# A fourth group in the second Q/K unit, a fifth in w_out's first and a seventh in w_down's last, with four more raw places and a later return of h

## The chip, the cores and the metric

The kernel runs on one core of one Trainium2 chip. The metric is the device time of one execution in microseconds (us), as the median of several runs; lower is better. PE is the matrix engine (PEld its weight loads), DVE the vector engine, ACT the scalar engine, POOL GpSimd and SP the sync engine, which here only issues transfers.

## The reference, cut to what matters

One layer of a hybrid decoder, on 256 tokens of width 2048, in float32:

```python
def hybrid_mixer(u, w_in, ..., w_out):
    proj = jnp.einsum('bsd,de->bse', u, w_in)
    z, xbc, dt_raw, q, k, v = jnp.split(proj, IN_SPLITS, axis=-1)
    ...
    y_mix = jnp.concatenate([y_ssm, y_att], axis=-1)
    return jnp.einsum('bse,ed->bsd', y_mix, w_out)

def squared_relu_mlp(u, w_up, w_down):
    hdn = jax.nn.relu(jnp.einsum('bsd,df->bsf', u, w_up))
    return jnp.einsum('bsf,fd->bsd', hdn * hdn, w_down)

h = h + rmsnorm(hybrid_mixer(rmsnorm(h, ...), ...), norm_mix_post[i])
h = h + rmsnorm(squared_relu_mlp(rmsnorm(h, ...), ...), norm_mlp_post[i])
```

y_ssm comes from a state-space scan (SSD, 32 heads), y_att from an attention of 16 heads. w_in is 2048 x 12320, w_out 4096 x 2048, w_up 2048 x 8192, w_down 8192 x 2048. The work around the change is in the products with w_in (the columns of q, k and v), w_out and w_down.

## The kernel before, in words

**Products in three parts.** PE multiplies in fp32r, which is less exact than float32. So each operand is split into a high part and a rest, x = hi + lo, and a product of float32 becomes three matmuls: hi by hi, hi by lo, lo by hi. The activations stay in SBUF, split, with the features on the partitions (`u` for the layer's input, called ua, ub and uc in a profile; `sh`, `sl` for y_ssm; `ah`, `al` for y_att, and later sh and ah hold the MLP's inner activations). The weights come from DRAM in raw tiles of 256 rows x 512 columns (512 KB), a "block" of k each: `fetch` and `fetch_next` (L149, L201) issue the load on SP's queue, `split` (L140) has ACT write hi (L144) and DVE write lo = raw - hi (L145). There are five pairs of hi and lo (BUFS). Raw tiles lie in a ring of four buffers (RAWS), to which `room["raw"]` adds places that other data do not need at that time; `room["turn"]` counts through the ring.

**Units and groups.** `unit` (L436) computes 256 tokens x two column blocks of 512, over a list of k blocks, in an order that is written out by hand. A *plain* block takes, for each column block, one raw tile and 2 token tiles x 2 k x 3 = 12 matmuls of 512 columns (`row_tile`, L325 to L327), 24 in all. A block *by seven* (a "group": `seven`, L372) uses Strassen's way of multiplying 2 x 2 blocks with seven products in place of eight: 7 x 3 = 21 matmuls (L408 to L410) into four more accumulators (`more`). It needs sums of weight tiles, which DVE adds (L249: e, of two tiles' size, and t4, of half), each split like a raw tile, so that four tiles are split (a, e, b and t, the last of half size); and sums of activations, which `sums_of_acts` (L354) makes once for each block of k and keeps in `room["sums"]`: four DVE additions (L365 to L368) and a split into hi and lo. In the tables of blocks this sum stands ahead of the block before the group. Of the second column block a group needs the sum of its two rows too: for w_out, w_up and w_down a pair of transfers on POOL's queue adds them up in DRAM ahead of time (`next_pair`, L264; the second transfer accumulates; five places, four ahead), and SP loads the sum; for w_in DVE adds them in place (raw<-raw). Behind a unit's last group a `combine` adds the four extra accumulators to the results, and a few plain blocks (`last`) close the unit, one column block after the other.

**Order.** The engines' queues are in program order. The loads and splits of weights have a high priority, so that they are placed as early as their buffers allow; `split_in_line` and `add_in_line` keep ACT's and DVE's part of them in the order of the blocks. `waiting` holds generators (attention, sums, copies), of which `pump` takes a step behind each block's column block.

**The three stages.** (1) The second Q/K unit, `keys_by_tokens(1, ...)`, takes heads 4 to 7 of q and k as its two column blocks. It starts when the SSD is done, whose memory becomes `ah` and `al` (16 feature blocks each). Their second halves hold the sums of activations at first; the first halves are empty until attention writes y_att there, behind the first V unit (`heads`). That V unit, `two_values(0, ...)`, comes next, with groups 1, 3, 5 and 6. (2) w_out's first unit takes columns 0 to 1023, blocks 5 to 15 (the first five are done before); its sums of activations are kept for the second unit, which uses block 9 too. (3) w_down's last unit, the second half of the inner features by columns 1024 to 2047, ends the kernel. In both of w_down's last units the layer's h lies in DRAM (`h_d`), so that its places (`ha`, `hb`) can hold raw tiles: the ring is 4 + 2 (uc) + 3 (ha) + 1 (hb) = 10 places in the unit before and 4 + 2 in the last. At the last unit's start `copies` brings h back on ACT's queue (8 transfers of 128 x 512, one a step), and `load_wpost` loads two of the norm's weights. Behind the last unit (`complete`, `finish`) h gets the MLP's normed output added and is stored.

Of the kernel before, what the change touches and what calls it, by code (L numbers as in the profile page):

```python
# [16 lines left out]
P = 128  # L17
S = 256
# [36 lines left out]
QK_SEVENS = (1, 3, 5)  # L55
# [22 lines left out]
def hymba_layer(ctx: ExitStack, tc: tile.TileContext, x, norm_mix_pre, w_in, conv_w, conv_b, dt_bias, a_log,  # L78
# [34 lines left out]
    def part(k):  # L113
        return (sh, sl, k) if k < NK else (att["h"], att["l"], k - NK)
# [74 lines left out]
    def beside_up(raws, turn):  # L189

        room["sums"] = [v[:, k:k + KB] for k in range(NK // 2, NK, KB) for v in (ah, al)]
# [67 lines left out]
    def plan(name, src, n, order, by_seven):  # L259

        orders[name, n] = order_of(order, by_seven)
        pairs.extend((src, n * NB, k) for k in order if k in by_seven)
# [162 lines left out]
    plan("out", w_out, 0, range(EARLY, 14), (6, 8, 10, 12))  # L425
# [8 lines left out]
    plan(("down", 1), w_downs[1], 2, (0, 1, 3, 2, 6, 4, 8, 5, 11, 7, 13, 9), (3, 6, 8, 11, 13, 9))  # L434
# [409 lines left out]
    def attention(ap, h, qT, kT, v):  # L844
# [39 lines left out]
        split(ah[:, h:h + 2], al[:, h:h + 2], o)  # L884
# [94 lines left out]
    ah = att["h"] = bigr.tile([P, NK, S], F32R, name="ah")  # L979
    al = att["l"] = bigr.tile([P, NK, S], F32R, name="al")  # L980
    ap_ = ExitStack()
    ap = ap_.enter_context(tc.tile_pool(name="ap", bufs=2, side="right", reuse_waits="tile"))
    room["sums"] = [v[:, k:k + KB] for k in range(NK // 2, NK, KB) for v in (ah, al)]
    room["raw"], room["turn"], room["acts"] = [], 0, act_u
# [5 lines left out]
    qk.append(keys_by_tokens(1, (0, 2, 1, 4, 3, 7, 5), (6,), *eight))  # L990
    vs = two_values(0, *eight[::-1])
    heads(0, *qk[0], vs[0])
# [233 lines left out]
    nc.scalar.activation(cp.tile([P, 1], F32, name="mean", bufs=2), al[:, NK - 1, 0:1].bitcast(F32), AF.Sqrt, scale=0.0, bias=ones[:, 0:1])  # L1226
# [4 lines left out]
    def new_h():  # L1231
        hs[:] = [hp.tile([P, NT, n * NB], F32, name=name) for n, name in ((3, "ha"), (1, "hb"))]
# [108 lines left out]
    def copies(dst, src, step):  # L1341

        for n in range(4):
# [82 lines left out]
    a, b = hp.tile([P, 3 * KB, NB], F32, name="ha"), hp.tile([P, KB, NB], F32, name="hb")  # L1426
    in_u = room["raw"]
    room["raw"] = [*in_u, *(a[:, k:k + KB] for k in range(0, 3 * KB, KB)), b]
# [5 lines left out]
    for n in (2, 3):  # L1434
        load_wpost(norm_mlp_post, n)
    new_h()
    room["raw"], room["turn"], room["chain"] = in_u, 0, False
    waiting.append(copies(of_h, in_dram, 1))
    unit(w_downs[1], 2, orders[("down", 1), 2], (10, 12, 14, 15), more, acc,
         lambda x: combine_onto(2, x), LAG_DOWN, (complete(2), finish))  # L1440
# [23 lines left out]
```

## Time and profile before

| what | us |
|---|---|
| median of 3 runs | 1460.41 (1460.25 to 1460.97) |
| the profiled execution | 1460.92 |
| its span, first to last instruction | 1459.0 |
| splits of raw tiles on ACT (L144, hi<-raw), 412, busy | 431.1 |
| the same on DVE (L145, lo<-raw,hi), 412, busy | 501.7 |
| raw tiles of w_in by SP, 181 of 512 KB, from issue to landing (median of one) | 3.8 |
| raw tiles of w_out by SP, 39 of 512 KB, from issue to landing (median of one) | 5.1 |
| sums of pairs for w_down by POOL, 48 of 256 KB, from issue to landing (median of one) | 6.1 |

The time of an execution is its span and 1.92 us around it. Busy times of different engines overlap, and an engine's busy time counts only as time of the kernel where the others wait for it. In the rows of a timeline the columns are start, length, engine, line, operation, out<-in, partitions x elements, count, and in brackets the idle time before the instruction with what ended it. In the windows the columns are named ahead of the rows.

### The profile page before, as it was taken

How to read it: one execution, taken by the hardware profiler on the slowest of the kernel's cores; microseconds unless marked ns; L12 is line 12 of the kernel's file. 1: busy time of each engine (PE TensorE's matmuls, PEld its weight loads, DVE VectorE, ACT ScalarE, POOL GpSimd, SP SyncE). 2: the span in 40 equal slices, each digit the busy share in tenths (PEclk: the TensorE clock that was granted, in tenths of full speed). 3: DMA queues.
4: the chain of work that ended last, by engine and by line, in shares of the span. 5: the costliest groups of instructions: out<-in, count | busy, mean ns of one | idle time of the engine just before them, and what ended most of it. 6: DMA issues, size and time to landing. Idle time of an engine off the chain costs nothing.

```text
span 1459.0 us, 20278 instructions
## 1 busy us (share of the span) xinstructions
PE 1451.0 (99%) x7126; PEld 1224.5 (84%) x7126; DVE 1257.1 (86%) x1865; ACT 892.2 (61%) x1220; POOL 143.5 (10%) x210
## 2 busy tenths in 40 slices
PE   9999999999999999999999999999999999999998
PEld 8888888888888888888888888888888888888886
DVE  6798897798887696689978999999888999999987
ACT  7465665465566556555657677666455776766553
POOL 0003100212010000000100011011101111101000
PEclk9999999999999999999999999999999999999999
DMA  8666666566887486688876798678889888798763
GB/s 266 210 204 180 187 175 198 177 174 186 229 233 218 130 245 197 190 261 261 245 225 214 205 313 244 199 225 252 243 241 283 251 245 246 208 307 239 252 212 116
DMA packets 168278, 324.06 MB, mean 222 GB/s; under 512 B 15232, under 2 KB 18160, under 8 KB 168176
## 3 DMA queue, kind: packets, MB, share of 16 engines
q1 hardware_dynamic: 144464, 272.37, 59.0%
q0 software_dynamic: 15840, 36.71, 12.4%
q10 hardware_dynamic: 7872, 13.68, 2.8%
q8 instruction: 56, 0.92, 0.2%
q14 instruction: 46, 0.38, 0.1%
HBM read 318.48 MB, written 40.93 MB: 246 GB/s over the span
## 4 chain that ended last, share of the span: by engine, by line
PE 99%; DVE 0%; ACT 0%; issue 0%; ACTq 0%
PE acc L470 15%; PE acc L325 12%; PE acc L327 12%; PE acc L326 12%; PE acc L473 8%; PE acc L410 6%; PE acc L408 6%; PE acc L409 6%; PE ps L325 3%; PE ps L327 3%; PE ps L326 3%; PE ps L410 2%; PE ps L408 2%; PE ps L409 2%; PE ps L804 1%; PE acc L1379 1%
## 5 line engine op out<-in xcount | busy, mean ns | idle before, releaser
L144 ACT ACTIVATE hi<-raw 128x1024 fp32r<-128x1024 f32 (+1 forms) x412 | 431.1, 1051 | 290.5 <-PE acc L327 102.3
L145 DVE TENSOR_TENSOR lo<-raw,hi 128x1024 fp32r<-128x1024 f32 (+1 forms) x412 | 501.7, 1221 | 103.9 <-ACT hi L144 99.9
L470 PE MATMUL acc<-ua,hi 128*128 128x512 f32 x600 | 163.7, 402 | 0.0
L470 PEld LDWEIGHTS acc<-ua,hi 128*128 128x128 f32 x600 | 106.0, 189 | 16.7
L144 ACT ACTIVATE hi<-e 128x1024 fp32r<-128x1024 f32 x62 | 65.9, 1063 | 72.2 <-DVE e L249 67.2
L325 PE MATMUL acc<-hi,ua 128*128 128x512 f32 x248 | 98.6, 397 | 0.0
L326 PE MATMUL acc<-lo,ua 128*128 128x512 f32 x248 | 96.8, 391 | 0.0
L327 PE MATMUL acc<-hi,ua 128*128 128x512 f32 x248 | 96.8, 390 | 0.0
L473 PEld LDWEIGHTS acc<-ua,lo 128*128 128x128 f32 x600 | 88.2, 190 | 10.2
L473 PE MATMUL acc<-ua,lo 128*128 128x256 f32 x600 | 90.8, 281 | 0.0
L325 PE MATMUL acc<-hi,sh 128*128 128x512 f32 x224 | 88.5, 395 | 0.0
L327 PE MATMUL acc<-hi,sl 128*128 128x512 f32 x224 | 87.4, 390 | 0.0
L326 PE MATMUL acc<-lo,sh 128*128 128x512 f32 x224 | 87.3, 390 | 0.0
L145 DVE TENSOR_TENSOR lo<-e,hi 128x1024 fp32r<-128x1024 f32 x62 | 75.5, 1218 | 0.0
L470 PE MATMUL acc<-uc,hi 128*128 128x512 f32 x240 | 68.5, 398 | 0.0
L408 PE MATMUL acc<-hi,ah 128*128 128x512 f32 x167 | 65.1, 390 | 0.0
L410 PE MATMUL acc<-hi,al 128*128 128x512 f32 x167 | 65.1, 390 | 0.0
L409 PE MATMUL acc<-lo,ah 128*128 128x512 f32 x167 | 65.1, 390 | 0.0
L327 PE MATMUL acc<-hi,al 128*128 128x512 f32 x144 | 56.1, 389 | 0.0
L326 PE MATMUL acc<-lo,ah 128*128 128x512 f32 x144 | 56.1, 389 | 0.0
L325 PE MATMUL acc<-hi,ah 128*128 128x512 f32 x144 | 56.0, 389 | 0.0
L327 PEld LDWEIGHTS acc<-hi,ua 128*128 128x128 f32 x248 | 46.6, 188 | 10.1
(533 smaller groups left out, 3437.2 us busy)
## 6 DMA issues: line engine op xcount, KB each, us to landing
raw<-in_w_in_dram SPq DMA_DIRECT2D x181, 512.0 KB, 3.8
raw<-in_w_down_dram SPq DMA_DIRECT2D x76, 512.0 KB, 4.9
raw<-in_w_up_dram SPq DMA_DIRECT2D x65, 512.0 KB, 4.7
raw<-in_w_out_dram SPq DMA_DIRECT2D x39, 512.0 KB, 5.1
pair<-in_w_up_dram POOLq DMA_DIRECT2D x56, 256.0 KB, 5.5
pair<-in_w_down_dram POOLq DMA_DIRECT2D x48, 256.0 KB, 6.1
raw<-pair SPq DMA_DIRECT2D x47, 256.0 KB, 4.4
ha<-in_w_up_dram SPq DMA_DIRECT2D x20, 512.0 KB, 5.3
```

The source lines that it names most:

```text
L144: return (nc.scalar.activation(hi, src, AF.Copy), nc.vector.tensor_tensor(lo, src, hi.bitcast(F32), op=ALU.subtract))
L145: nc.vector.tensor_tensor(lo, src, hi.bitcast(F32), op=ALU.subtract))
L325: nc.tensor.matmul(dst, a_h[:, r, ts], hi[:, j], start=begin and j == 0, stop=False)
L326: nc.tensor.matmul(dst, a_h[:, r, ts], lo[:, j], start=False, stop=False)
L327: product[t] = nc.tensor.matmul(dst, a_l[:, r, ts], hi[:, j], start=False, stop=end and j == KB - 1)
L408: nc.tensor.matmul(dst, a_h, hi[:, j], start=own and first, stop=False)
L409: nc.tensor.matmul(dst, a_h, lo[:, j], start=False, stop=False)
L410: nc.tensor.matmul(dst, a_l, hi[:, j], start=False, stop=own and last)
L470: nc.tensor.matmul(acc[f], hi[:, j, f * P:(f + 1) * P], u(k0 + j), start=k0 + j == 0, stop=False, skip_group_check=True)
L473: nc.tensor.matmul(acc[f][:, 0], lo[:, j, f * P:(f + 1) * P], u(k0 + j)[:, 0], start=False, stop=k0 + j == NK - 1, skip_group_check=True)
L804: nc.tensor.matmul(p[:, c, r], bc[:, r, c * P:(c + 1) * P], xdt[:, c, r], start=True, stop=True)
L1379: nc.tensor.transpose(p[:, f * P:(f + 1) * P], r[:, f * P:(f + 1) * P], ident)
```

## The change

It alters the number and the order of groups in three units, and the places that make this possible.

In the second Q/K unit the groups are 1, 3, 5 and 6 in place of 1, 3 and 5, in the order 0 2 1 3 4 5 6 | 7 (before 0 2 1 4 3 7 5 | 6). `ah` and `al` become two halves each: ah1 and al1, with the sums, and the first halves, which are allocated twice: as `not_yet`, four more raw places (a ring of eight) for this unit and the first V unit, and behind that as `att[0]` for y_att. `part` finds the half of a feature block.

In w_out's first unit the groups are 6, 8, 9, 10 and 12, in the order 5 6 7 8 9 11 10 13 12 | 14 15 (before 6, 8, 10, 12 in 5 to 13 | 14 15).

In w_down's last unit the groups are 3, 6, 8, 11, 13, 9 and 12, in the order 0 1 3 2 6 8 4 11 13 5 9 12 | 7 10 14 15 (before six, 0 1 3 2 6 4 8 5 11 7 13 9 | 10 12 14 15). Block 12 has no sum of activations yet; `hb` becomes the place for it and is a raw place no more. The ring, now 4 + 2 + 3 = 9 places, is kept through the last unit's groups. `onto_and_h` takes the place of the combine behind the last group: it combines, and only then allocates h, loads the two norm weights, cuts the ring to 4 + 2, and queues the copies of h, two a step.

```diff
@@ -52,7 +52,7 @@
 FIRST = 3
 UP_SEVENS = (1, 3, 4, 6)
 V_SEVENS = (1, 3, 5, 6)
-QK_SEVENS = (1, 3, 5)
+QK_SEVENS = (1, 3, 5, 6)
 PAIRS_AHEAD = 4
 
 
@@ -111,7 +111,10 @@
     att = {}
 
     def part(k):
-        return (sh, sl, k) if k < NK else (att["h"], att["l"], k - NK)
+        if k < NK:
+            return sh, sl, k
+        i, r = divmod(k - NK, NK // 2)
+        return (*att[i], r)
 
 
     mid = ExitStack()
@@ -188,7 +191,7 @@
 
     def beside_up(raws, turn):
 
-        room["sums"] = [v[:, k:k + KB] for k in range(NK // 2, NK, KB) for v in (ah, al)]
+        room["sums"] = [v[:, k:k + KB] for k in range(0, NK // 2, KB) for v in att[1]]
         b = hp.tile([P, NT, NB], F32, name="hb")
         room["shared"] = [[b[:, t] for t in range(NT)],
                           [hp.tile([P, NB], F32, name="wpost", bufs=2) for _ in range(NT)]]
@@ -422,7 +425,7 @@
 
     for n in (0, 2):
         plan("v", w_v, n, range(7), V_SEVENS)
-    plan("out", w_out, 0, range(EARLY, 14), (6, 8, 10, 12))
+    plan("out", w_out, 0, (5, 6, 7, 8, 9, 11, 10, 13, 12), (6, 8, 9, 10, 12))
     plan("out", w_out, 2, (0, 6, 1, 9, 2, 12, 3, 4, 5, 8, 7, 10), (6, 9, 12, 4, 8, 10))
     for hf in range(2):
         for n in range(0 if hf else 2, 8, 2):
@@ -431,7 +434,7 @@
             plan(("down", 0), w_down, 0, (0,1,2,4,3,6,5,9,7,10,8,11,12,13), (4,6,9,10,11,13))
             plan(("down", 0), w_down, 2, (0, 4, 1, 6, 2, 9, 3, 11, 5, 13, 7, 10, 8), (4, 6, 9, 11, 13, 10))
     plan(("down", 1), w_downs[1], 0, (0, 1, 2, 3, 4, 6, 5, 8, 7, 9, 10, 11, 12, 13), (3, 6, 8, 9, 11, 13))
-    plan(("down", 1), w_downs[1], 2, (0, 1, 3, 2, 6, 4, 8, 5, 11, 7, 13, 9), (3, 6, 8, 11, 13, 9))
+    plan(("down", 1), w_downs[1], 2, (0, 1, 3, 2, 6, 8, 4, 11, 13, 5, 9, 12), (3, 6, 8, 11, 13, 9, 12))
 
     def unit(src, n, order, last, acc, more, combine, lag=0, at_end=(None, None), first=True, ending=None,
              ready=None):
@@ -881,7 +884,8 @@
             for j, pT in enumerate(pair):
                 nc.tensor.matmul(o[:, j], v[:, 0, j], pT[:, :S], start=True, stop=False, skip_group_check=True)
                 nc.tensor.matmul(o[:, j, P:], v[:, 1, j], pT[:, S:], start=False, stop=True, skip_group_check=True)
-        split(ah[:, h:h + 2], al[:, h:h + 2], o)
+        d_h, d_l, i = part(NK + h)
+        split(d_h[:, i:i + 2], d_l[:, i:i + 2], o)
 
     def queries(c0, scale, pumps=(1,)):
         acc = gemm_features(w_in, c0, pumps=pumps)
@@ -976,19 +980,21 @@
     drain()
     ssd.close()
     bigr = ctx.enter_context(tc.tile_pool(name="bigr", bufs=1, side="right", reuse_waits="tile"))
-    ah = att["h"] = bigr.tile([P, NK, S], F32R, name="ah")
-    al = att["l"] = bigr.tile([P, NK, S], F32R, name="al")
+    att[1] = [bigr.tile([P, NK // 2, S], F32R, name=name) for name in ("ah1", "al1")]
+    not_yet = [bigr.tile([P, 2 * KB, NB], F32, name=name) for name in ("ah0", "al0")]
     ap_ = ExitStack()
     ap = ap_.enter_context(tc.tile_pool(name="ap", bufs=2, side="right", reuse_waits="tile"))
-    room["sums"] = [v[:, k:k + KB] for k in range(NK // 2, NK, KB) for v in (ah, al)]
-    room["raw"], room["turn"], room["acts"] = [], 0, act_u
+    room["sums"] = [v[:, k:k + KB] for k in range(0, NK // 2, KB) for v in att[1]]
+    room["raw"], room["turn"], room["acts"] = [t[:, k:k + KB] for t in not_yet for k in (0, KB)], 0, act_u
     waiting.append(sums_ahead())
     with tc.high_priority(offset=AHEAD):
         for _ in range(PAIRS_AHEAD):
             next_pair()
     eight = eight_banks()
-    qk.append(keys_by_tokens(1, (0, 2, 1, 4, 3, 7, 5), (6,), *eight))
+    qk.append(keys_by_tokens(1, (0, 2, 1, 3, 4, 5, 6), (7,), *eight))
     vs = two_values(0, *eight[::-1])
+    room["raw"], room["turn"] = [], 0
+    att[0] = [bigr.tile([P, NK // 2, S], F32R, name=name) for name in ("ah0", "al0")]
     heads(0, *qk[0], vs[0])
     q2 = queries(COL_Q + 2 * NB, rbq, (1,0,1,1,0,1,1,1))
     drain()
@@ -1223,13 +1229,13 @@
                       fetch=fetch_next)
     assert not waiting
     ap_.close()
-    nc.scalar.activation(cp.tile([P, 1], F32, name="mean", bufs=2), al[:, NK - 1, 0:1].bitcast(F32), AF.Sqrt, scale=0.0, bias=ones[:, 0:1])
+    nc.scalar.activation(cp.tile([P, 1], F32, name="mean", bufs=2), att[1][1][:, NK // 2 - 1, 0:1].bitcast(F32), AF.Sqrt, scale=0.0, bias=ones[:, 0:1])
     mid.close()
     hp = ctx.enter_context(tc.tile_pool(name="hp", bufs=1, reuse_waits="tile"))
     hs = []
 
-    def new_h():
-        hs[:] = [hp.tile([P, NT, n * NB], F32, name=name) for n, name in ((3, "ha"), (1, "hb"))]
+    def new_h(n=2):
+        hs[:] = [hp.tile([P, NT, n * NB], F32, name=name) for n, name in ((3, "ha"), (1, "hb"))[:n]]
 
     def of_h(t, cs):
 
@@ -1338,9 +1344,9 @@
             nc.vector.tensor_tensor(m, acc, m, op=ALU.subtract if n % 2 else ALU.add)
         return at_end
 
-    def copies(dst, src, step):
-
-        for n in range(4):
+    def copies(dst, src, step, blocks=range(4)):
+
+        for n in blocks:
             for t in range(NT):
                 with tc.issue_after((line.get("act") or product[1]).ins):
                     nc.scalar.dma_start(dst(t, columns(n)), src(t, columns(n)))
@@ -1423,21 +1429,29 @@
         return at_end
 
     in_place_of_u()
-    a, b = hp.tile([P, 3 * KB, NB], F32, name="ha"), hp.tile([P, KB, NB], F32, name="hb")
+    a, b = hp.tile([P, 3 * KB, NB], F32, name="ha"), hp.tile([P, KB, 2, S], F32R, name="hb")
     in_u = room["raw"]
-    room["raw"] = [*in_u, *(a[:, k:k + KB] for k in range(0, 3 * KB, KB)), b]
+    room["raw"] = [*in_u, *(a[:, k:k + KB] for k in range(0, 3 * KB, KB))]
+    room["sums"] += [b[:, k] for k in range(KB)]
     room["chain"] = True
     for n in range(2):
         load_wpost(norm_mlp_post, n)
     unit(w_downs[1], 0, orders[("down", 1), 0], (14, 15), acc, more,
          lambda x: combine_onto(0, x), 0, (complete(0), complete(1)))
-    for n in (2, 3):
-        load_wpost(norm_mlp_post, n)
-    new_h()
-    room["raw"], room["turn"], room["chain"] = in_u, 0, False
-    waiting.append(copies(of_h, in_dram, 1))
-    unit(w_downs[1], 2, orders[("down", 1), 2], (10, 12, 14, 15), more, acc,
-         lambda x: combine_onto(2, x), LAG_DOWN, (complete(2), finish))
+    room["chain"] = False
+
+    def onto_and_h(more):
+
+        combine_onto(2, more)
+        new_h()
+        for n in (2, 3):
+            load_wpost(norm_mlp_post, n)
+        n = room["turn"] % (RAWS + len(room["raw"]))
+        room["raw"], room["turn"] = in_u, min(n, RAWS + len(in_u)) % (RAWS + len(in_u))
+        waiting.append(copies(of_h, in_dram, 2))
+
+    unit(w_downs[1], 2, orders[("down", 1), 2], (7, 10, 14, 15), more, acc,
+         onto_and_h, LAG_DOWN, (complete(2), finish))
 
 
 # ---- launch: one core; inputs and outputs as the reference has them ----
```

Three places show what moves. First DVE in the second Q/K unit, from group 1's last split (lo<-tk) on. Before:

```order
L145 TENSOR_TENSOR lo<-tk,hi 128x512
L145 TENSOR_TENSOR lo<-raw,hi 128x1024 x2
L249 TENSOR_TENSOR raw<-raw 128x512
L249 TENSOR_TENSOR cT<-raw 128x512
L249 TENSOR_TENSOR cT<-cT,raw 128x512
```

And of the change:

```order
L148 TENSOR_TENSOR lo<-tk,hi 128x512
L252 TENSOR_TENSOR al_3683<-al_3683 128x512
L252 TENSOR_TENSOR cT<-al_3683 128x512
L252 TENSOR_TENSOR cT<-cT,al_3683 128x512
L148 TENSOR_TENSOR lo<-al_3683,hi 128x1024
```

The two splits of plain block 4 no longer stand between the groups 1 and 3, and group 3's raw tile lies in a place of the first half of al (cT holds e, tk holds t4 here).

Second, DVE in w_out's first unit, from group 8's b split on. Before, where a sum of activations (r<-ah,al and the three behind it) and a plain block follow it:

```order
L145 TENSOR_TENSOR lo<-raw,hi 128x1024
L145 TENSOR_TENSOR lo<-r,hi 128x512
L365 TENSOR_TENSOR r<-ah,al 128x512
L366 TENSOR_TENSOR r<-r 128x256
L367 TENSOR_TENSOR r<-r 128x128
L368 TENSOR_TENSOR r<-r 128x128
L145 TENSOR_TENSOR lo<-raw,hi 128x1024
L145 TENSOR_TENSOR ua<-r,ua 128x512
L145 TENSOR_TENSOR lo<-raw,hi 128x1024
L249 TENSOR_TENSOR e<-uc 128x512
```

And of the change, where group 9 follows it:

```order
L148 TENSOR_TENSOR lo<-raw,hi 128x1024
L148 TENSOR_TENSOR lo<-r,hi 128x512
L252 TENSOR_TENSOR e<-raw 128x512
L252 TENSOR_TENSOR e<-e,raw 128x512
L148 TENSOR_TENSOR lo<-raw,hi 128x1024
L252 TENSOR_TENSOR r<-e,raw 128x512
L148 TENSOR_TENSOR lo<-e,hi 128x1024
L148 TENSOR_TENSOR lo<-raw,hi 128x1024
L148 TENSOR_TENSOR lo<-r,hi 128x512
L368 TENSOR_TENSOR r<-ah_4431,al_4432 128x512
L148 TENSOR_TENSOR lo<-uc,hi 128x1024
```

The seven operations of group 9 stand ahead of the next sum, which is block 10's (the same operations as before's sum, which was block 10's too).

Third, ACT in w_down's last unit. Before, the copies of h (ha<-h_d, hb<-h_d) stand in it from the unit's start on:

```order
L144 ACTIVATE hi<-raw 128x1024 x2
L1346 DMA ha<-h_d 128x512 x2
L144 ACTIVATE hi<-raw 128x1024
L1346 DMA ha<-h_d 128x512
L144 ACTIVATE hi<-raw 128x1024
L1346 DMA ha<-h_d 128x512 x3
L144 ACTIVATE hi<-uc 128x1024
L1419 ACTIVATE junk,ssq<-mw_6119 128x512
L1346 DMA hb<-h_d 128x512
```

And of the change, behind the combine's L1045, among the splits of the last four blocks:

```order
L1045 ACTIVATE r<-ps 128x512
L147 ACTIVATE hi<-raw 128x1024
L1352 DMA ha<-h_d 128x512
L147 ACTIVATE hi<-raw 128x1024 x2
L147 ACTIVATE hi<-uc 128x1024
L1352 DMA ha<-h_d 128x512 x2
L147 ACTIVATE hi<-uc 128x1024
L1352 DMA ha<-h_d 128x512 x3
L147 ACTIVATE hi<-raw 128x1024
L1352 DMA hb<-h_d 128x512 x2
L147 ACTIVATE hi<-raw 128x1024
```

The eight copies have moved behind the last group; only one of the unit's hi splits comes after the last of them.

## The prediction

> **What bounds the kernel now.** I read the page first, then the waits of the matrix engine, then the three changed stages by windows, then timelines inside them. From the page, with the chain's shares by engine as its last line here:
>
> ```profile
> span 1459.0 us, 20278 instructions
> ...
> PE 1451.0 (99%) x7126; PEld 1224.5 (84%) x7126; DVE 1257.1 (86%) x1865; ACT 892.2 (61%) x1220; POOL 143.5 (10%) x210
> ...
> PE 99%; DVE 0%; ACT 0%; issue 0%; ACTq 0%
> ```
>
> The chain that ended last is PE for 99%. The waits of PE, as total, times and longest:
>
> ```profile
> PE ps L1324 <- ACT dg L1323: 1.7, 1, 1.7
> PE ps L521 <- DVE half L510: 1.1, 1, 1.1
> PE acc L1102 <- DVE ha L1093: 0.2, 1, 0.2
> ```
>
> None of these lines belongs to a unit that is changed. The windows of the second Q/K unit, of w_out's first unit and of w_down's last (us, then busy time of PE, PEld, DVE, ACT, POOL, then granted clock, DMA share, GB/s):
>
> ```profile
> 360.77:404.98 44.21, 44.21 (x197) 36.59 (x196) 39.34 (x52) 25.01 (x29) 6.06 (x8) 1.00 0.86 241
> 628.95:691.51 62.56, 62.56 (x277) 51.81 (x276) 55.50 (x71) 35.38 (x44) 6.31 (x10) 1.00 0.83 250
> 1367.24:1445.92 78.68, 78.68 (x349) 65.15 (x348) 67.87 (x85) 43.55 (x54) 0.17 (x1) 1.00 0.58 196
> ```
>
> PE is busy through all three at clock 1.00. So the time falls by what PE has less to do, as long as DVE, second in line, keeps up.
>
> **What a group saves.** I write S3 for block 3 done by seven and R4 for block 4 done plainly. The first matmul of S1, of the plain block behind it and of S3, in the Q/K unit:
>
> ```profile
> 371.68 0.39 PE L408 MATMUL ps<-hi,ua 128*128 128x512 f32 x1
> ...
> 376.44 0.39 PE L325 MATMUL acc<-hi,ua 128*128 128x512 f32 x1
> ...
> 381.88 0.39 PE L408 MATMUL ps<-hi,ua 128*128 128x512 f32 x1
> ```
>
> 21 matmuls take 4.76 us and 24 take 5.44: 0.227 us each, start to start. The 0.39 us of a row is one matmul's latency, part of which the next one overlaps; with it the saving would come out too large. Three blocks turn from plain to seven, 9 matmuls fewer: 9 x 0.227 = **2.04 us**.
>
> The Trainium skill bears on this number (TensorE: Matmul & The Clock Gate, section Back-to-back issue gap): it gives about 131 ns per matmul for a sustained stream of 512 columns, by which 9 matmuls would be 1.2 us, and about 216 ns for an isolated one. The trace's 227 ns over whole blocks is near the second, and decides.
>
> **What the groups cost DVE in Q/K.** A seven adds up weight tiles and splits four of them (a, e, b, t) in place of two. The starts of S1's last split, then S3's first addition, its e and t splits, then S5's first addition, e and t:
>
> ```profile
> 369.94 0.69 DVE L145 TENSOR_TENSOR lo<-tk,hi 128x512 fp32r<-128x512 f32 x1
> ...
> 375.54 0.69 DVE L249 TENSOR_TENSOR raw<-raw 128x512 f32<-128x512 f32 x1
> ...
> 379.34 1.22 DVE L145 TENSOR_TENSOR lo<-cT,hi 128x1024 fp32r<-128x1024 f32 x1
> ...
> 381.61 0.68 DVE L145 TENSOR_TENSOR lo<-tk,hi 128x512 fp32r<-128x512 f32 x1
> ...
> 389.70 1.22 DVE L145 TENSOR_TENSOR lo<-cT,hi 128x1024 fp32r<-128x1024 f32 x1
> ```
>
> From 375.54 to 382.21 (381.61 plus 0.60, the pitch of such an operation) is 6.67 us for a seven, against PE's 4.76: a seven directly behind a seven eats 1.91 us of the lead, by which I mean the time from the end of a split to PE's first use of it. S3 is now behind S1. S1's last split ends at 370.63; S3's e split comes 5.02 later (380.56 less 375.54), at 375.65, and PE, with S3 at 376.44, wants it at its eighth matmul, 378.03: lead 2.4, or 2.0 with the waits for a free hi/lo pair. S5 has R4 ahead of it and keeps its lead. PE starts its second matmul, for which the a tile must be ready, at
>
> ```profile
> L409 PE MATMUL ps<-lo,ub x1: 389/389/389, 392.3 to 392.3; 128*128 128x512 f32 x1
> ```
>
> and its eighth 1.36 later, at 393.66; the e split ends at 390.92: 2.74. S6 directly behind S5 is left with 2.74 - 1.91 = **0.83**. No wait, but it is the tightest point of this stage. By shares it is tight as well: a seven for a plain block (two splits of 1.13) adds 4.41 to DVE's 39.34, which makes 43.75 in 43.53 us of stage. What DVE lacks comes out of the lead.
>
> The data must be there too. Of the stage's loads, the two of the fourth block in order (R4's, whose turn S3 now has):
>
> ```profile
> L158 SPq DMA_DIRECT2D raw<-in_w_in_dram x2: 368/368/368, 357.1 to 359.6; - x2
> ...
> DMA to landing us min/median/max: 6.2/6.3/6.4
> ```
>
> They landed by 366.0, and S3's additions want them from 370.6: in time by 4.6 us even with four places. The four more let the loads behind them go out as soon as SP's queue reaches them. Free places must wait for the last reader of what lay there, the SSD's transposes, which end before 350 and hold nothing up:
>
> ```profile
> L824 PE MATMUL ps<-ident,yg x8: 271/272/273, 345.9 to 349.5; 128*128 128x128 f32 x8
> ```
>
> So the loads cost nothing; some of them move from after 365 to before it.
>
> **w_out's first unit.** S9 follows S8, and block 9's sum of activations moves here from the second unit. DVE around S8, from the split before it, and then PE's first use of S8's a tile:
>
> ```profile
> 635.75 1.23 DVE L145 TENSOR_TENSOR lo<-uc,hi 128x1024 fp32r<-128x1024 f32 x1 [1.94 <-ACT hi L144]
> ...
> 638.63 0.68 DVE L249 TENSOR_TENSOR e<-raw 128x512 f32<-128x512 f32 x1
> ...
> 641.69 1.22 DVE L145 TENSOR_TENSOR lo<-e,hi 128x1024 fp32r<-128x1024 f32 x1
> ...
> 644.57 0.68 DVE L365 TENSOR_TENSOR r<-ah,al 128x512 f32<-128x512 f32 x1
> ...
> 646.28 1.22 DVE L145 TENSOR_TENSOR lo<-raw,hi 128x1024 fp32r<-128x1024 f32 x1
> 647.41 0.69 DVE L145 TENSOR_TENSOR ua<-r,ua 128x512 fp32r<-128x512 f32 x1
> 648.02 1.22 DVE L145 TENSOR_TENSOR lo<-raw,hi 128x1024 fp32r<-128x1024 f32 x1
> ```
>
> ```profile
> 644.82 0.39 PE L409 MATMUL ps<-lo,ah 128*128 128x512 f32 x1
> ```
>
> A seven with a pair from DRAM is 5.94 us (638.63 to 644.57), a sum 1.71 + 0.61 = 2.32. S8's e tile is ready at 642.91 and read six matmuls after its a tile, at 646.18: lead 3.27. In the new order 0.71 of the moved sum falls into the 1.94 us in which DVE waited, and 1.61 stands ahead of the e tile, less some 0.4, since operations that now alternate don't wait for one another: 2.06 is left. S9 eats 5.94 - 4.76 = 1.18 of it: **0.9**; R11, with block 10's sum ahead of it, gets about as little. From there a seven, a sum and a plain block cost DVE 10.52 and PE 10.20 as before, and the last four halves restore the lead. By shares: 55.50 + 3.68 + 2.32 = 61.5 of 61.88.
>
> **w_down's last unit.** Three adjacent pairs: S6 S8, S11 S13, S9 S12, and a new sum. The same form is there already, since S9 directly follows S13, and the smallest lead that stalled nothing is there too:
>
> ```profile
> 1381.03 2.36 DVE L145 TENSOR_TENSOR lo<-raw,hi 128x1024 fp32r<-128x1024 f32 x2 [1.57 <-ACT hi L144]
> ...
> 1386.37 1.22 DVE L145 TENSOR_TENSOR lo<-e,hi 128x1024 fp32r<-128x1024 f32 x1
> ...
> 1422.02 1.22 DVE L145 TENSOR_TENSOR lo<-e,hi 128x1024 fp32r<-128x1024 f32 x1
> ```
>
> ```profile
> 1383.11 0.39 PE L326 MATMUL acc<-lo,sh 128*128 128x512 f32 x1
> ...
> 1425.27 0.39 PE L409 MATMUL acc<-lo,ua 128*128 128x512 f32 x1
> ```
>
> S9's e tile keeps 2.03 (1425.27 less 1423.24). The plain block behind S3 had 0.86 (1383.11 less 1382.25, the end of the first of the two splits). S6's e tile ends at 1387.59 and is read 30 matmuls after 1383.11, at 1389.91: 2.32, so S8 keeps some 1.15; S12, behind S9 with about 2.2, some 1.05. The ring's loss of a place costs nothing: the DMA share here is 0.58.
>
> **h's return.** Eight copies and two small loads move from the unit's start to behind the last group, into ACT's order between the last splits. A copy that must wait holds ACT, and behind it every hi, DVE's lo and PE. ACT's own last splits, with its wait before each, DVE's first use of h, and the landing of the copies as they are now:
>
> ```profile
> 1434.09 1.06 ACT L144 ACTIVATE hi<-raw 128x1024 fp32r<-128x1024 f32 x1 [1.66 <-PE acc L327]
> 1436.81 1.07 ACT L144 ACTIVATE hi<-raw 128x1024 fp32r<-128x1024 f32 x1 [1.66 <-PE acc L327]
> ...
> 1447.10 2.21 DVE L1330 SCALAR_TENSOR_TENSOR ha<-mw,rff,ha 128x512 f32<-128x512 f32 x4
> ...
> DMA to landing us min/median/max: 3.1/6.1/9.9
> ```
>
> The last two copies go out ahead of the last hi, by 1436.8; at 9.9 us they land at 1446.7, before 1447.10. ACT waits for PE 1.66 us before each late split, which covers two issues. Price nothing; without that cover at most the lateness of a copy, worked out below. The two more pair sums on POOL and its DMAs lie in queues that wait for nobody here; the extra hi splits are ACT's, idle for over 40% of each window.
>
> The **sum**: 1460.92 (the profiled run, span 1459.0 and 1.92 around it) - 2.04 = 1458.88. The median of the runs shown is 1460.41, 0.51 less, so I predict **1458.4 us**.
>
> **Rivals.**
>
> *A, partly lost.* My leads at four points (S6 in Q/K; S9 and R11 in w_out; S12) are 0.8 to 1.05. Were DVE later there by 1 to 1.5 us, PE would wait 0.2 to 0.6 at each: 0.8 to 2.0, time 1459.2 to 1460.4. For it: DVE's shares are full in two stages. Against: 0.86 stalled nothing.
>
> *B, slower: DVE becomes the bound of the three stages.* Place: each seven directly behind another. Were the lead on entry 0.86, the lowest row, instead of 2.0 to 3.3, PE would wait 1.05 for S3 and again for S6, and 0.32 for each of the four other adjacent pairs: 3.4; the two sums, not hidden, 4.6 more. The time would be 1460.41 - 2.04 + 3.4 to 8.0 = 1461.8 to 1466.4. It decides from the point where the waits pass 2.04, an entry lead of about 1 with half a sum uncovered. Against it: the entry leads worked out above are 2 or more.
>
> *C, h late.* The first copy waits for the last splits from the places of h. A seven's worth of backlog (5.94) on DVE would hold ACT that long, less a lead of 2 to 4: 2 to 4 us, or 1460.4 to 1462.4. Against: those splits stand ahead of the copy by two of ACT's.
>
> *D, the matmul rule.* With 131 ns each, in the sentence above, 1459.2.
>
> *E, the gain is larger.* PE is idle for 8.0 us of the span. Were h's later copy to let its start or its tail end 1 us sooner, 1457.4. Against: no row shows a wait of that kind, and PE's listed waits add up to 3.0.
>
> **How the numbers follow.** Forecast 0.60, A 0.18, B 0.13, C 0.04, D 0.02, E 0.03. The range goes from 1457.3 to 1461.3: it holds the forecast with 0.8 of spread, A, D, and the lower ends of C; B's most and E's half are left out. Less than 0.2% (2.9 us) can't be told from no change here, so the forecast itself counts as the same: faster needs 1457.5 (E and a tail of the forecast, 0.06), slower needs 1463.3 (most of B, a little of C, 0.12), the same 0.82.
>
> **What would show it.** Right: 9 matmuls of 512 columns fewer, no new line in PE's waits, the three windows shorter by 0.68 each, DVE busy over 97% in the first two, its smallest lead 0.8 to 1. Wrong: PE waiting at L409 or L326 for DVE's lo (A, B), or ACT's last splits later than 1437 and the tail waiting for h (C).

## The result, and the profile after

The changed kernel takes 1458.59 us (median of 21 runs, 1457.81 to 1460.1), the kernel before beside it 1461.12 (21 runs, 1459.83 to 1463.18). The ratio is 0.9983, with a 95% interval of 0.9977 to 0.9989: 2.5 us less, between 1.6 and 3.4. Forecast were 1458.4, and 2.04 less. The page of the profile after, from its head, and its chain by engines:

```profile
span 1456.6 us, 20308 instructions
...
PE 1448.5 (99%) x7117; PEld 1222.2 (84%) x7117; DVE 1268.3 (87%) x1886; ACT 897.8 (62%) x1227; POOL 146.2 (10%) x214
...
PE 99%; DVE 0%; ACT 0%; issue 0%; ACTq 0%
```

PE has 9 instructions less (7126 before) and is busy for 2.5 us less; DVE is busy for 11 us more. The waits of PE (total, times, longest):

```profile
PE ps L1330 <- ACT dg L1329: 1.7, 1, 1.7
PE ps L524 <- DVE half L513: 1.1, 1, 1.1
PE acc L1108 <- DVE ha L1099: 0.2, 1, 0.2
```

They are the three of before, at lines that have moved by 3 to 6, and no new one. The windows over the same three stages, cut at the same matmuls as before (to 0.03 us):

```profile
360.39:403.94 43.55, 43.55 (x194) 36.03 (x193) 42.74 (x58) 26.01 (x30) 7.39 (x11) 1.00 0.89 246
627.91:689.79 61.88, 61.88 (x274) 51.24 (x273) 58.54 (x79) 37.74 (x47) 7.33 (x11) 1.00 0.83 250
1365.40:1443.39 77.99, 77.99 (x346) 64.58 (x345) 72.90 (x95) 46.03 (x57) 0.91 (x2) 1.00 0.59 189
```

They were 44.21, 62.56 and 78.68 us long, so they are 0.66, 0.68 and 0.69 shorter, with three PE instructions less in each. PE is still busy without a gap. DVE is busy for 98%, 95% and 93% of them, where it was 89%, 89% and 86%.

The same can be followed through the whole execution. Certain matmuls (mostly transposes) stand behind the stages in both kernels; this is how much later (+) or earlier (-) a stage between two of them ends in a profile than in the profile of before, in us (differences of start times in the traces, each less the one ahead of it):

| kernel | first 8 us | to 109 | with the Q/K unit (to 405) | with w_out (to 768) | to 1242 | w_down's two last units (to 1450) |
|---|---|---|---|---|---|---|
| the change | -0.31 | -0.07 | **-0.66** | **-0.68** | -0.12 | **-0.69** |
| the change, again | -0.44 | 0.00 | -0.66 | -0.68 | -0.10 | -0.66 |
| Q/K alone | -0.80 | -0.02 | **-0.68** | 0.00 | -0.18 | +0.05 |
| w_out alone | -0.72 | +0.02 | 0.00 | **-0.68** | -0.12 | +0.05 |
| w_down alone | +1.52 | -0.07 | 0.00 | +0.13 | -0.10 | **-0.63** |
| ring of four | -0.44 | -0.07 | +2.10 | +0.54 | -0.18 | -0.63 |
| out triple | -0.51 | -0.05 | -0.68 | +1.06 | -0.12 | -0.65 |
| Q/K four in a row | -0.55 | -0.05 | +2.97 | -1.18 | -0.09 | -0.70 |
| h early | +0.21 | -0.05 | -0.67 | -0.68 | -0.03 | +1.31 |
| ring cut | -0.27 | 0.00 | -0.68 | -0.68 | -0.05 | +0.30 |
| one more group | +0.89 | -0.08 | -0.68 | -0.68 | -0.11 | -0.83 |
| one more, spread | -0.87 | +0.12 | -0.68 | -0.68 | -0.05 | **-1.36** |

Read along a row, a stage that is not touched keeps its length within 0.2, mostly within 0.1. The exception is the first column: the start of the kernel scatters by over 2 us between executions, more than a whole group of the change brings. It explains why single times, and medians of ten, say less than the columns do. But each row is one profiled execution: where a stage hangs on when a load lands, as with the ring of four, h early and the ring cut, another execution may lose more or less.

How close DVE is to PE can be read in pairs of rows: the split of a tile on DVE, and the matmul that first needs it. The e tile of S6 in Q/K, the e tile of S9 and the first tile of R11 in w_out, and the e tile of S12 and the first tile of R7 in w_down:

```profile
390.39 1.22 DVE L148 TENSOR_TENSOR lo<-cT,hi 128x1024 fp32r<-128x1024 f32 x1
...
647.81 1.22 DVE L148 TENSOR_TENSOR lo<-e,hi 128x1024 fp32r<-128x1024 f32 x1
...
651.29 1.22 DVE L148 TENSOR_TENSOR lo<-uc,hi 128x1024 fp32r<-128x1024 f32 x1
...
1420.49 1.22 DVE L148 TENSOR_TENSOR lo<-e,hi 128x1024 fp32r<-128x1024 f32 x1
...
1423.97 1.22 DVE L148 TENSOR_TENSOR lo<-raw,hi 128x1024 fp32r<-128x1024 f32 x1
```

```profile
392.63 0.39 PE L412 MATMUL acc<-lo,ah 128*128 128x512 f32 x1
...
649.90 0.39 PE L412 MATMUL acc<-lo,ua 128*128 128x512 f32 x1
...
653.30 0.39 PE L329 MATMUL acc<-lo,ah 128*128 128x512 f32 x1
...
1422.74 0.39 PE L412 MATMUL acc<-lo,hb 128*128 128x512 f32 x1
...
1426.14 0.39 PE L329 MATMUL acc<-lo,sh 128*128 128x512 f32 x1
```

The split's start plus 1.22 is its end; what is left until the matmul is the lead: 1.02, 0.87, 0.79, 1.03 and 0.95 us. None is used up, and none has much to spare.

### The profile page after: what moved, and what is told of

Same layout as the page of the kernel before. It is cut to its first block, busy times and chain, and to the rows that moved or that the text cites. A ratio compares the mean times of both kernels' runs of the same rounds, so it can differ in the third digit from the quotient of the medians.

```text
span 1456.6 us, 20308 instructions
## 1 busy us (share of the span) xinstructions
PE 1448.5 (99%) x7117; PEld 1222.2 (84%) x7117; DVE 1268.3 (87%) x1886; ACT 897.8 (62%) x1227; POOL 146.2 (10%) x214
## 4 chain that ended last, share of the span: by engine, by line
PE 99%; DVE 0%; ACT 0%; issue 0%; ACTq 0%
PE acc L473 15%; PE acc L328 12%; PE acc L330 12%; PE acc L329 12%; PE acc L476 8%; PE acc L413 6%; PE acc L411 6%; PE acc L412 6%; PE ps L330 3%; PE ps L329 3%; PE ps L328 3%; PE ps L413 2%; PE ps L411 2%; PE ps L412 2%; PE ps L807 1%; PE acc L1385 1%
## 5 line engine op out<-in xcount | busy, mean ns | idle before, releaser
L147 ACT ACTIVATE hi<-raw 128x1024 fp32r<-128x1024 f32 (+1 forms) x392 | 409.8, 1051 | 268.6 <-PE acc L473 92.2
L148 DVE TENSOR_TENSOR lo<-raw,hi 128x1024 fp32r<-128x1024 f32 (+1 forms) x392 | 476.9, 1221 | 92.7 <-ACT hi L147 88.7
L411 PE MATMUL acc<-hi,ah 128*128 128x512 f32 x174 | 67.8, 389 | 0.0
L412 PE MATMUL acc<-lo,ah 128*128 128x512 f32 x174 | 67.7, 389 | 0.0
L413 PE MATMUL acc<-hi,al 128*128 128x512 f32 x174 | 67.7, 389 | 0.0
L148 DVE TENSOR_TENSOR lo<-ha,hi 128x1024 fp32r<-128x1024 f32 x43 | 52.4, 1220 | 6.0 <-ACT hi L147 5.7
L147 ACT ACTIVATE hi<-ha 128x1024 fp32r<-128x1024 f32 x43 | 45.3, 1057 | 18.3 <-PE acc L330 9.8
L330 PEld LDWEIGHTS acc<-hi,ua 128*128 128x128 f32 x248 | 46.6, 188 | 10.0
L328 PEld LDWEIGHTS acc<-hi,ua 128*128 128x128 f32 x248 | 46.6, 188 | 9.4 <-ACT ua L149 0.3
```

Of the source, the lines that this page charges most:

```text
L147: return (nc.scalar.activation(hi, src, AF.Copy), nc.vector.tensor_tensor(lo, src, hi.bitcast(F32), op=ALU.subtract))
L148: nc.vector.tensor_tensor(lo, src, hi.bitcast(F32), op=ALU.subtract))
L328: nc.tensor.matmul(dst, a_h[:, r, ts], hi[:, j], start=begin and j == 0, stop=False)
L330: product[t] = nc.tensor.matmul(dst, a_l[:, r, ts], hi[:, j], start=False, stop=end and j == KB - 1)
L411: nc.tensor.matmul(dst, a_h, hi[:, j], start=own and first, stop=False)
L412: nc.tensor.matmul(dst, a_h, lo[:, j], start=False, stop=False)
```

## The experiments

All are compared with runs of the kernel before on the same chip, and with the table above.

**Each part alone.** Three kernels hold the change in one place only and the kernel before elsewhere. The edit of the second one, as the shortest:

```diff
-    plan("out", w_out, 0, range(EARLY, 14), (6, 8, 10, 12))
+    plan("out", w_out, 0, (5, 6, 7, 8, 9, 11, 10, 13, 12), (6, 8, 9, 10, 12))
```

> The kernel before with the Q/K part of the change alone (fourth group, its order, four raw places); w_out and w_down as before. Theory (three matmuls fewer, no wait): the time between the start of this unit and its end is 0.68 us shorter than before, every other stage keeps its length, time about 0.7 us below before. Rival A/B (DVE runs out of lead here): less than 0.3 us gained or a loss, with PE waiting at L412 for a split of block 6. By a matmul price of 131 ns the unit would be 0.39 us shorter.

> The kernel before with w_out's first unit alone changed (five groups). Theory: that unit 0.68 us shorter, the rest unchanged, smallest lead of DVE 0.8 to 0.9 behind group 9. Rival: PE waits for group 9 or block 11, gain under 0.3 us. By 131 ns a matmul 0.39 us.

> The kernel before with w_down's part alone changed (seventh group, hb for sums, ring of 9 kept, h back behind the last group). Theory: last unit 0.68 us shorter, the tail behind it unchanged. Rival C (h late): the tail longer by 1 us or more, the copies of h landing after DVE's first use. By 131 ns a matmul 0.39 us.

Measured: 1459.61, 1460.64 and 1460.26 us, against 1460.98 before; ratios 0.9988 (0.9979 to 0.9998), 0.9998 (0.9988 to 1.0007) and 0.9996 (0.9987 to 1.0005). Of the times only the first is clear of no change, since a part is worth a quarter of what an interval spans. The stages decide: 0.68, 0.68 and 0.63 us shorter where the part is, and unchanged elsewhere. That is 0.21 to 0.23 us for each of three matmuls. By the 131 ns that the Trainium skill gives for a sustained stream (TensorE: Matmul & The Clock Gate, section Back-to-back issue gap) it would be an estimated 0.39, which these stages do not bear out. Neither A nor B came about in any part. C did not either: in the third the tail behind the unit is 9.0 us long, against 8.8 before, but it is 9.0 in w_out alone too, where nothing of it was altered.

**The ring of four.** The changed kernel without its four raw places in Q/K:

```diff
-    not_yet = [bigr.tile([P, 2 * KB, NB], F32, name=name) for name in ("ah0", "al0")]
...
-    room["raw"], room["turn"], room["acts"] = [t[:, k:k + KB] for t in not_yet for k in (0, KB)], 0, act_u
+    room["raw"], room["turn"], room["acts"] = [], 0, act_u
```

> The changed kernel without the four extra raw places: the Q/K unit and the first V unit run on the ring of four, in the new order. Theory of the prediction (S3's data is in time with four places too): no PE wait at group 3, time 1458.6, at most 0.5 more. Rival (the places carry this group): the loads for groups 5 and 6 go out later, DVE's additions wait for a DMA, and PE waits 1 to 3 us in this unit: 1459.6 to 1461.6.

Measured: 1461.69 us, ratio 1.0004 (0.9994 to 1.0013); the Q/K unit 2.10 us longer than before in place of 0.66 shorter, and 1.2 more lost until w_out's end. S3 had its data in time. Here are DVE's first additions of S5 and of S6, and then PE's first use of the a tiles of S5 and S6:

```profile
383.40 0.69 DVE L252 TENSOR_TENSOR raw<-raw 128x512 f32<-128x512 f32 x1 [3.54 <-DMA raw<-in_w_in_dram]
...
390.07 0.68 DVE L252 TENSOR_TENSOR raw<-raw 128x512 f32<-128x512 f32 x1
```

```profile
386.73 0.50 PE L412 MATMUL ps<-lo,ub 128*128 128x512 f32 x1 [0.21 <-DVE lo L148]
...
393.40 0.50 PE L412 MATMUL ps<-lo,uc 128*128 128x512 f32 x1 [1.24 <-DVE lo L148]
```

DVE sat idle for 3.54 us until a raw tile of S5 had landed (issued at 376.6, landed at 383.3; in the changed kernel the same load was issued at 359.3 and landed at 367.2). That used up the lead, so that S6, directly behind, was late again by most of what an adjacent group costs DVE over PE. S6's own tiles were there by 385.8, before its first addition. The rival holds, but with one load in place of two: the four places carry this group by S5's load, and neither by S3's nor by S6's.

**Adjacent groups.** If the lead is what counts, a third and a fourth group in a row must cost a time that can be worked out. Two edits of the changed kernel's orders, each with the same groups:

```diff
-    plan("out", w_out, 0, (5, 6, 7, 8, 9, 11, 10, 13, 12), (6, 8, 9, 10, 12))
+    plan("out", w_out, 0, (5, 6, 7, 8, 9, 10, 11, 13, 12), (6, 8, 9, 10, 12))
```

```diff
-    qk.append(keys_by_tokens(1, (0, 2, 1, 3, 4, 5, 6), (7,), *eight))
+    qk.append(keys_by_tokens(1, (0, 2, 4, 1, 3, 5, 6), (7,), *eight))
```

> The changed kernel with w_out's first unit in the order 5 6 7 8 9 10 11 13 12: the same groups, but 8, 9 and 10 directly behind one another. Theory (a seven behind a seven eats 1.18 us of DVE's lead, a sum some 2 us more, and PE waits for what is missing): group 9's smallest lead is gone (0.87 less 1.4), group 10 lacks 2.3 us, so PE waits about 2.3 us in this unit and the time is about 1460.9. Rival (only the count of matmuls matters, or ACT and the ring limit before DVE does): 1458.6, no wait.

> The changed kernel with the Q/K unit in the order 0 2 4 1 3 5 6 | 7: four groups in a row. Theory: from group 3's smallest lead of 2.04 us each further group eats 1.91: group 5 is left with 0.13, no wait; group 6 lacks 1.78, so PE waits about 1.8 us and the time is about 1460.4. Rival: 1458.6 without a wait, or data-limited with DVE's additions waiting for a DMA and more than 3 us lost.

Measured: 1459.99 us (ratio 0.9990, 0.9981 to 1.0000) and 1461.48 (1.0000, 0.9991 to 1.0010). In the triple the stage is 1.06 longer than before where the change is 0.68 shorter: 1.74 of wait, where 2.3 were expected. In the row of four, S5 still came without a wait (its e tile had 0.14 left, 0.13 expected). What PE then waited for, in the triple at S10, and in the row of four at S6 and at the second half of the last block:

```profile
653.45 0.39 PE L411 MATMUL acc<-hi,ah 128*128 128x512 f32 x1
654.93 0.50 PE L411 MATMUL acc<-hi,ua 128*128 128x512 f32 x1 [1.10 <-ACT hi L147]
655.27 0.40 PE L412 MATMUL ps<-lo,ah 128*128 128x512 f32 x1
```

```profile
390.85 0.39 PE L411 MATMUL ps<-hi,uc 128*128 128x512 f32 x1
391.08 0.39 PE L411 MATMUL acc<-hi,uc 128*128 128x512 f32 x1
392.51 0.50 PE L411 MATMUL acc<-hi,ah 128*128 128x512 f32 x1 [1.04 <-ACT hi L147]
...
404.97 0.50 PE L329 MATMUL ps<-lo,ua 128*128 128x512 f32 x1 [1.46 <-DVE lo L148]
```

The engine named is ACT. Its split ahead of that matmul, in the triple and then in the row of four:

```profile
653.83 1.06 ACT L147 ACTIVATE hi<-e 128x1024 fp32r<-128x1024 f32 x1 [2.94 <-DVE e L252]
```

```profile
391.40 1.06 ACT L147 ACTIVATE hi<-cT 128x1024 fp32r<-128x1024 f32 x1 [3.18 <-DVE cT L252]
```

ACT stood idle for some 3 us until DVE had added up the tile e (cT in Q/K): the engine that is late is DVE. The rows show something else that I had not counted on: around the late tiles PE's own order differs from the changed kernel's. There the matmuls of a group come as L411 (hi by hi), L412 (with the lo), L413 throughout these two stages. Here, at eight places in the triple's stage and nine in and behind the row of four, one hi by hi follows another, and the matmuls with the lo come later. So these two edits change more than the order of blocks. The sum of leads assumes the order of the changed kernel, in which a late lo holds PE at once; what the other order did to the waits was not tested. The second wait of the row of four I had not foreseen. On DVE:

```profile
400.54 2.12 DVE L943 TENSOR_TENSOR tk<-acc,tk 128x512 f32<-128x512 f32 x3
403.10 0.69 DVE L943 TENSOR_TENSOR tk<-acc,tk 128x512 f32<-128x512 f32 x1 [0.44 <-PE acc L330]
403.70 2.35 DVE L148 TENSOR_TENSOR lo<-raw,hi 128x1024 fp32r<-128x1024 f32 x2
```

The unit's final additions wait for PE's last accumulator, and the next unit's splits stand behind them on DVE; with the lead gone, PE in turn waits for such a split. In all this unit lost 3.6 us against the change, and gained 0.5 back in the next.

**h early, and the ring alone.** The first edit puts the copies of three column blocks and the norm weights back to the unit's start; the second only cuts the ring there, with all copies left late:

```diff
-    room["chain"] = False
+    for n in (2, 3):
+        load_wpost(norm_mlp_post, n)
+    new_h(1)
+    room["raw"], room["turn"], room["chain"] = in_u, 0, False
+    waiting.append(copies(of_h, in_dram, 1, range(3)))
...
```

```diff
-    room["chain"] = False
+    room["raw"], room["turn"], room["chain"] = in_u, 0, False
...
```

> The changed kernel with h's copies for its first three column blocks, and the two norm weights, back at the start of w_down's last unit as before, so that unit runs on a ring of 4 + 2; only the last column block's copy (hb) comes behind the last group. Theory of the prediction (neither the ring's places nor the moment of the copies carries the time): the unit as long as in the changed kernel, 1458.6, with DVE's smallest leads 0.9 at block 2 and 1.15 at group 8. Rival (the kept ring is what feeds the adjacent groups): PE waits 0.5 to 2 us in this unit, 1459.1 to 1460.6.

> The changed kernel with the ring cut to 4 + 2 at the start of w_down's last unit, as before the change, but with h's copies and the norm weights still behind the last group. It tells the ring from the copies, which the experiment with h early changed together (2.1 us lost there at block 2, behind a load that landed late). Theory 1 (the ring carries it: the loads go out when a place is free): the same wait of about 2 us at block 2, 1460.2 or more. Theory 2 (the copies and norm weights carry it, by their place in ACT's order and by the DMAs they take): no wait at block 2, 1458.6.

Measured: 1460.23 us (0.9988, 0.9979 to 0.9998) and 1459.58 (0.9988, 0.9979 to 0.9997). In the profiles the unit loses 2.0 us against the change with h early, and 1.0 with the ring cut alone. PE's new waits, all at block 2, with h early and then with the ring cut:

```profile
PE acc L329 <- DVE lo L148: 0.8, 1, 0.8
PE acc L328 <- ACT hi L147: 0.7, 1, 0.7
```

```profile
PE acc L329 <- DVE lo L148: 0.6, 1, 0.6
```

ACT's split of the tile that is late, in the kernel with h early, and then with the ring cut:

```profile
1367.63 1.06 ACT L147 ACTIVATE hi<-raw 128x1024 fp32r<-128x1024 f32 x1 [5.80 <-DMA raw<-in_w_down_dram]
```

```profile
1366.08 1.06 ACT L147 ACTIVATE hi<-raw 128x1024 fp32r<-128x1024 f32 x1 [4.67 <-DMA raw<-in_w_down_dram]
```

Where the ring is cut, its count starts again at the four raw buffers, and the next load waits until one is read; with the copies on top it lands later still (8.2 us from issue to landing, 7.0 with the ring cut alone). PE then waits at block 2, and S8 keeps a smallest lead of 0.48 us in place of 2.04 (0.47 with the ring cut alone). So in these two profiles each theory has about half: 1.0 us for the ring and another 1.0 for the copies' late return. The times agree with the ring's part: 1459.58 against 1458.36 for the changed kernel on the same chip (below). The copies' part rests on one profile. Both kernels stand at the same ratio to the kernel before, and two of the ten executions of h early (1457.98 and 1458.19) are as fast as the changed kernel, so the loss is not in every execution. How the copies would do it is not shown either; what ACT's row names is the load, and not a copy.

**One more group.** In w_down's unit before the last block 12 can be done by seven as well, since the change has made a place for its sum. The first order keeps groups 11 and 12 next to each other; the second spreads the groups and takes a plain block from the unit's end to ahead of the last group:

```diff
-    plan(("down", 1), w_downs[1], 0, (0, 1, 2, 3, 4, 6, 5, 8, 7, 9, 10, 11, 12, 13), (3, 6, 8, 9, 11, 13))
+    plan(("down", 1), w_downs[1], 0, (0, 1, 3, 2, 6, 4, 8, 5, 9, 7, 11, 12, 10, 13), (3, 6, 8, 9, 11, 12, 13))
```

```diff
+    plan(("down", 1), w_downs[1], 0, (0, 1, 3, 2, 6, 4, 8, 5, 9, 7, 11, 10, 12, 14, 13), (3, 6, 8, 9, 11, 12, 13))
...
-    unit(w_downs[1], 0, orders[("down", 1), 0], (14, 15), acc, more,
+    unit(w_downs[1], 0, orders[("down", 1), 0], (15,), acc, more,
```

> The changed kernel with block 12 by seven in w_down's unit before the last too (seven groups there; its sum of activations moves there, so it is no more work in the last unit): three matmuls fewer again. Theory (DVE's lead is spent in this unit: its smallest leads are 1.5 to 2.1 at its end, and the group and the sum cost DVE 6.0 us more): PE waits 2 to 4 us, time 1460 to 1462. Rival (DVE still has room, as its busy share of 87% says): 0.68 less, 1457.9.

> The kernel of the one-more-group experiment with the groups of w_down's unit before the last spread out: 0 1 3 2 6 4 8 5 9 7 11 10 12 14 13 | 15, so that a plain block stands between any two groups and one more of them ahead of the last. There PE waited 0.5 us around the adjacent groups 11 and 12. Theory (DVE lacks only that much, and a plain block gives its lead 3.2 us): no wait, this unit and the last together 0.68 us shorter than in the changed kernel, time 1457.9. Rival (DVE is full over the whole unit, so that the wait only moves to the last group): as the one-more-group kernel, 0.1 to 0.2 us below the changed one. Second rival (the combine now has two halves in place of four to finish in): PE waits at the last unit's first matmul, slower than the changed kernel.

> The changed kernel once more, on the same chip as the spread-out version, so that these two can be compared run for run. It should read 1458.6, the same 2.0 to 2.5 us below the kernel before, and its stages 0.68 us shorter in each of the three places.

Measured: 1458.28 us for the first (0.9975, 0.9966 to 0.9984), where I expected 2 to 4 us of wait. The group gave 0.14: its stage loses some 0.5 us of the 0.68 around S12 and S13, where the leads come down to 0.05 to 0.2. The spread order gives 1457.15 us (7 runs, 1456.87 to 1457.38; 0.9972, 0.9961 to 0.9983), the changed kernel on the same chip 1458.36 (11 runs, 1458.01 to 1458.62): 1.2 us less, and the two ranges don't meet. Its stage is 1.36 shorter than before, twice the change's. Its waits of PE:

```profile
PE ps L1330 <- ACT dg L1329: 1.7, 1, 1.7
PE ps L524 <- DVE half L513: 1.1, 1, 1.1
PE acc L1108 <- DVE ha L1099: 0.2, 1, 0.2
```

No new one. This is the fastest of the kernels. 0.68 of the 1.2 are the group. The rest is not explained: in its profile the first 8 us are 0.4 shorter than in the changed kernel's on the same chip, and the tail behind the last unit is 0.4 shorter too (8.6 us in both kernels with this group, 8.8 to 9.0 in all others).

My theory on this failed in one step: I took the lead at the unit's end, 1.5 to 2.1 us, for all that DVE had. But lead is also lost where several plain blocks follow one another. In the changed kernel the unit ends with four halves of plain blocks and the next begins with two more; the lead rose to over 8 us there, and then DVE waited, because all five pairs of hi and lo were full and ACT could not go on until PE had read one. ACT's row, and then DVE's:

```profile
1376.62 1.06 ACT L147 ACTIVATE hi<-ha 128x1024 fp32r<-128x1024 f32 x1 [1.19 <-PE acc L330]
```

```profile
1377.71 2.45 DVE L148 TENSOR_TENSOR lo<-ha,hi 128x1024 fp32r<-128x1024 f32 x2 [1.56 <-ACT hi L147]
```

In the spread kernel that wait is gone. DVE's waits for hi over both units (1285 to 1445), in the changed kernel and in the spread one:

```profile
DVE lo L148 <- ACT hi L147: 2.6, 4, 1.6
```

```profile
DVE lo L148 <- ACT hi L147: 1.0, 3, 0.4
```

That is one part of what pays for the group; the plain block that was moved ahead of the last group is another, and how they share it was not measured.

## Why the prediction was right, and where it was not

**The saving: right.** 9 matmuls at 0.227 us were to bring 2.04; the three stages are 2.03 shorter in sum, and the three parts alone show 0.63 to 0.68 each. The other 0.5 of the measured 2.5 are not shown to be part of the change: in the profiles 0.38 of it lie ahead of the Q/K unit, where nothing was altered and the first 8 us scatter, and the median of before moved from 1460.41 to 1461.12 with more runs. So it is in part luck that 1458.4 came within 0.2 us of the measured time: the base that I started from was 0.71 low, and the fall was 0.49 larger than forecast. I also wrote that less than 0.2% can't be told from no change; with 21 runs of each, 0.17% could.

**The leads: right where the data were there.** S6 in Q/K was to keep 0.83 and kept 1.02, S9 0.9 and 0.87, R11 about as little and 0.79, S12 1.05 and 1.03. That these leads decide was shown by the triple and the row of four, where the same sum, carried on in a longer row, said which group would miss, and its size within 0.6 us for the triple, though PE's order had changed there as well. For the row of four it named S6 rightly, but missed the second wait, which doubled the loss. For S8 in w_down I had 1.15, and it kept 2.04; the point on h's return says why.

**DVE's shares: too high.** I expected 43.75 and 61.5 us of busy time in the first two stages, over 97% in both; they were 42.74 and 58.54, which is 98% and 95%. In the second stage I added a group in place of a plain block and a sum, which are ten operations more, and the window has only eight more (79, where it was 71). Besides, the records of operations that follow closely overlap (a split of 1.22 us is followed after 1.13), and independent operations that alternate follow each other more closely (below), for which I had allowed 0.4 us at one place only. How these share the difference was not worked out.

**The loads of Q/K: a step that was wrong, without harm to the time.** I wrote that S3's data come in time "even with four places" and that the places cost nothing. The first is so. But I looked at S3 alone. Without the places S5 waits for its load, S6 behind it is late in turn, and the unit loses 2.8 us. The four places are a condition of this group, not an addition to it.

**h's return: a cost of nothing, but also a gain I had not seen.** The last two copies went out at 1431.6, landed 4.6 us later at most, and were first used at

```profile
1446.69 0.75 DVE L1336 SCALAR_TENSOR_TENSOR hb<-r,rff,hb 128x512 f32<-128x512 f32 x1
```

The cover was 10 us, where I had 0.4 at the worst landing. (I had set the last copies against the first use of ha, at 1447.10; they bring hb, whose first use came 2.1 us later.) What I did not price at all, the ring that is kept through the unit, is worth about 1 us: with the ring cut S8's lead falls to 0.47. The late copies are worth another 1.0 in one profile, in which the unit with its seven groups is slower than the old one with six; the times do not confirm it.

**The rivals.** A, B and C did not come about. A and B's mechanism is real all the same: it takes one group more in a row in w_out (1.7 us) and two more in Q/K (3.6 us). The kernel with the ring cut comes nearest to B's condition: S6 enters with 1.65 us there, and S8 behind it is left with 0.47, the 1.18 less that I had worked out. D is excluded by the stages of the three parts. E, the start or tail ending sooner, was given a chance for the wrong reason; the start does move by a microsecond, but up and down and without regard to the change.

## What to carry to other kernels

Where one engine is busy without a gap, price a cut in its work by its start-to-start pitch, and then follow the second engine's lead from tile to tile: it says which order of the same work is free and which is not, when a share of 87% says neither. A lead is limited by the buffers between the two engines, so it is worth trying light blocks between the heavy ones in place of a row of them at a unit's ends, as the spread order did, the fastest here. Places that "cost nothing" are to be tested by taking them away: here the extra raw places carried 2.8 us of their unit, and the ring that was kept about 1 us.

## What the runs showed of the hardware that was not expected

- The start of the kernel scatters. The second four transposes of x began at 7.48 us in the fastest profile and at 9.87 in the slowest (8.35 plus 1.52), for the same work; in four profiles PE waited 0.2 to 0.7 us for the load of x, and the rest of the difference has no row of its own.
- DVE follows an independent operation more closely than a dependent one. In the triple, S9's two additions of e alternate with those of a sum, and S10's two follow each other, the second needing the first:

```profile
645.14 0.68 DVE L252 TENSOR_TENSOR e<-raw 128x512 f32<-128x512 f32 x1
645.75 0.42 DVE L369 TENSOR_TENSOR r<-r 128x256 f32<-128x256 f32 x1
...
652.30 0.68 DVE L252 TENSOR_TENSOR e<-uc 128x512 f32<-128x512 f32 x1
653.02 0.69 DVE L252 TENSOR_TENSOR e<-e,uc 128x512 f32<-128x512 f32 x1
```

  The next operation starts 0.61 us behind the addition in the one case, 0.72 in the other. By these rows an order in which two chains alternate would give DVE an estimated tenth of a microsecond an operation.
- After a wait PE needs about 0.11 us more than its pitch: the matmul behind the one that waited starts 0.33 to 0.34 us later and not 0.227 (654.93 and 655.27 in the triple; 392.51 and 392.84, 404.97 and 405.31 in the row of four). So a wait costs more than its row in the list of waits says: the triple's one listed wait is 1.1, and its stage lost 1.74, with an unlisted wait of 0.13 at S9 and two late starts of this kind among it.
